# A one-core hybrid decoder step: one down sum per group, down loads two steps ahead, earlier first weights, preloaded residual rows

## The chip, the core and the metric

The kernel runs on one core of a Trainium2 chip. A core has five engines with queues of their own: the TensorE (PE; weight loads show as PEld) multiplies matrices into PSUM, the VectorE (DVE), the ScalarE (ACT) and GpSimd (POOL) work on elements, and the SyncE (SP) here issues every DMA. Each engine takes its instructions in a fixed order; what it reads from another engine or from a DMA it waits for by a semaphore. The metric is the device time of one execution in microseconds (us); lower is better.

## What is computed

One step of a decoder layer on 1104 tokens: 16 learned meta tokens and a prompt of 1024 as one sequence, and 8 samples of 8 tokens. A token mixer (a gated short convolution and a state-space part) is followed by an output projection, and then a feed-forward block (FFN). The end of the layer is what matters here:

```python
    mix = jnp.concatenate([ya, yb], axis=-1) @ w_out
    h = h + rmsnorm(mix, norm_mix_post)
    fn = rmsnorm(h, norm_ffn_pre)
    f = (jax.nn.silu(fn @ w_gate) * (fn @ w_up)) @ w_down
    h = h + rmsnorm(f, norm_ffn_post)
```

All is float32; the width is 1024, the FFN's 2816.

## The kernel before

**Products.** A float32 matrix product is made of three products of rounded halves: an operand is split into `hi` (an ACT copy into a rounded type) and `lo` (operand minus `hi`, a `tensor_tensor` on DVE or POOL), and PE computes hi·hi + hi·lo + lo·hi. So each weight needs a load, an ACT copy and a subtraction ahead of its use.

**Order of instructions.** A planner orders each engine's queue at build time, by its own estimate of times and by priorities: an instruction's place in the program, moved ahead by n places within `tc.high_priority(offset=n)`. Tiles of a pool with the same `tag` share `bufs` slots; a tile waits until the slot's last user is done. A pool that is opened after another was closed takes over its memory and waits for the tiles that lay there. The order is fixed on the chip: an instruction at the head of a queue holds everything behind it.

**Stages that the change touches.**

1. *Output projection* (lines 923 to 959). Three groups of token tiles, `GROUPS = ((1, 2, 3), (4, 9, 5), (6, 7, 8))`; tiles 1 to 8 are 128 prompt tokens each, 9 the samples. For each group twelve slices of `w_out` are loaded (`wo`), scaled and split (`woh`, `wol`) and multiplied. `load_mix` loads and splits the other operand (`mhb`, `mlb` and so on). After a group `h_tile` copies its sums out of PSUM; `residual` norms them and adds the input rows (line 868); `fn_tile` norms again, transposes on PE and fills `xr` and `B1`, the FFN's input. Both run within the next group; those of the last group run with the first FFN products.
2. *FFN up* (lines 964 to 1150). Gate and up weights (`g`, `u`) are taken in `NQ = 11` groups of 256 columns. A fast scheme for block matrices (Strassen, Winograd's form) makes seven products of 2 × 2 blocks: `first(q)` computes the products with B11 and B21 (two each for g and u), `rest(q)` the other five (T2, T3, T1, T4, B22; ten with g and u). The combinations of input blocks, the *B sums*, are made once (lines 1127 to 1137), those of the weights by `sums` in each group. `first` runs ahead for groups 0 to 2 (`ND = 3`) with weights of its own from `early_weights`; from group 3 on it is part of the group. PE's row "yg L982 <- DVE u2g" is a wait in `rest`: the accumulator Y is read by the DVE (`u2`, `u3`, lines 1048 and 1052) before the next product is added to it.
3. *Down sums* (`down_sums`, lines 1088 to 1097). For each group 1 MB of `w_down` is loaded into `xr[q % 2][0]` (row `xr<-in_w_down_dram`), POOL makes four sums in place, and the result is stored in DRAM as `d_t[q]`.
4. *Down projection* (lines 1154 to 1339): 42 steps, seven products with six batches of blocks each, in the order 1, 2, 6, 7, 4, 5, 3. `load(i)` loads and splits step i's operands; `draw()` hands out four half buffers in turn. Products 6, 7, 4 and 5 read `d_t`.
5. *Finish* (`finish_half`): a sum of squares on ACT, the product with the weight of the norm, the power −0.5 on POOL, and for each half row the residual `d_h` loaded into one of three buffers, added and stored.

## Time and profile before

| | us |
|---|---|
| median of 3 runs | 1493.08 (1485.3 to 1493.22) |
| the profiled execution | 1492.86 |
| its span, first to last instruction | 1490.9 |
| TensorE busy | 1399.4 |
| DVE, ACT, POOL busy | 921.0, 607.7, 563.2 |
| mean granted clock of the TensorE | 0.980 |

In the rows of the profile `L982 PE MATMUL xg<-B01h,a11g` means line 982, engine, operation, what it writes and what it reads, buffer numbers left out. A row of a group ends with the count, the busy time and the mean nanoseconds of one, and behind the last bar with the idle time ahead of it and what ended that. A row of the timeline begins with the start and the duration; brackets hold the idle time ahead of it and its releaser. In a row of stretches each engine has its busy time and, in parentheses, its instructions; then come the granted clock (1.00 is full), the mean share of time that the DMA engines were busy, and GB/s.

### The profile page before, as it was taken

The page shows a single profiled execution, that of the slowest core. Times are in us where ns is not written, and L with a number is a line of the kernel's source. Part 1 is how long each engine was busy: PE and PEld are TensorE (multiplying, and loading weights), DVE is VectorE, ACT ScalarE, POOL GpSimd, SP SyncE. Part 2 cuts the span into 40 slices and gives each one's busy share as a digit, 9 for nine tenths or more (in the row PEclk, how much of TensorE's full clock was granted, in tenths as well). Part 3 has the DMA queues.
Part 4 walks back from the last instruction along what each step waited for, and adds up shares of the span by engine and source line. Part 5 has one row for each costly group of instructions (what it writes and reads, how often), then busy time and mean ns, then how long its engine had stood idle before and what let it go on. Part 6 is the DMA issues. An engine that isn't in the chain of part 4 may idle for free.

```text
span 1490.9 us, 22203 instructions
## 1 busy us (share of the span) xinstructions
PE 1399.4 (94%) x8837; PEld 1267.5 (85%) x8837; DVE 921.0 (62%) x1050; ACT 607.7 (41%) x966; POOL 563.2 (38%) x404
## 2 busy tenths in 40 slices
PE   5999998989999889999989898999999999899996
PEld 5899987878898777787879888999999998687885
DVE  6555455656666976577499786665665545345654
ACT  5465444334433544565454222333333334343331
POOL 3122133434344453221157677222222233344442
PEclk9999999999999999999999999999999999999998
DMA  7143247667646557864434777432322357555445
GB/s 215 46 117 102 89 130 192 186 157 207 167 130 170 141 150 245 255 214 162 151 114 163 277 277 270 137 99 89 101 87 73 109 146 243 180 169 180 166 166 190
DMA packets 243696, 240.98 MB, mean 162 GB/s; under 512 B 32589, under 2 KB 193441, under 8 KB 242185
## 3 DMA queue, kind: packets, MB, share of 16 engines
q1 hardware_dynamic: 243592, 239.57, 51.5%
q8 instruction: 69, 1.13, 0.3%
q14 instruction: 35, 0.28, 0.1%
HBM read 170.81 MB, written 68.72 MB: 161 GB/s over the span
## 4 chain that ended last, share of the span: by engine, by line
PE 42%; DVE 6%; DMA 4%; issue 3%; ACT 2%; POOL 1%; SPq 0%; DVEq 0%; ACTq 0%; POOLq 0%
PE d L1306 11%; PE o L949 6%; PE yg L982 5%; PE yu L982 5%; PE xu L982 4%; PE xg L982 3%; PE zg L982 3%; PE zu L982 3%; DMA wg<-in_w_gate_dram 1%; DMA wu<-in_w_up_dram 1%; DMA c_p<-d_h 1%; PE d1s L1317 0%; DMA c_h<-d_h 0%; PE fT L896 0%; DVE c_p L1250 0%
## 5 line engine op out<-in xcount | busy, mean ns | idle before, releaser
L105 POOL TENSOR_TENSOR wd<-draw,wd 128x1024 fp32r<-128x1024 f32 (+1 forms) x41 | 98.8, 2413 | 118.8 <-ACT wd L1185 101.8
L218 PE MATMUL px<-xh,whi 128*128 128x272 f32 (+2 forms) x288 | 95.5, 333 | 0.0
L219 PE MATMUL px<-xl,whi 128*128 128x272 f32 (+2 forms) x288 | 94.9, 330 | 0.0
L220 PE MATMUL px<-xh,wlo 128*128 128x448 f32 (+2 forms) x288 | 94.2, 331 | 0.0
L105 POOL TENSOR_TENSOR wlo<-raw,whi 128x1024 fp32r<-128x1024 f32 x20 | 50.4, 2518 | 78.3 <-ACT whi L113 78.2
L252 DVE SCALAR_TENSOR_TENSOR xa<-xr,vec,xa 128x1040 f32<-128x1040 f32 x72 | 56.8, 846 | 33.9 <-issue 25.2
L941 DVE SCALAR_TENSOR_TENSOR wol<-wo,vec,woh 128x1024 fp32r<-128x1024 f32 x34 | 44.1, 1299 | 50.6 <-ACT woh L940 50.6
L1185 ACT ACTIVATE wd<-draw 128x1024 fp32r<-128x1024 f32 (+1 forms) x42 | 41.2, 984 | 80.5 <-DMA draw<-d_t 28.9
L218 PE MATMUL pz<-xh,whi 128*128 128x256 f32 (+2 forms) x192 | 67.7, 353 | 0.8 <-DVE z L594 0.7
L113 ACT ACTIVATE whi<-raw 128x1024 fp32r<-128x1024 f32 x38 | 40.1, 1055 | 62.0 <-PE px L219 20.3
L219 PE MATMUL pz<-xl,whi 128*128 128x256 f32 (+2 forms) x192 | 64.8, 338 | 0.0
L220 PE MATMUL pz<-xh,wlo 128*128 128x256 f32 (+2 forms) x192 | 64.8, 338 | 0.0
L940 ACT ACTIVATE woh<-wo,vec 128x1024 fp32r<-128x1024 f32 x34 | 38.8, 1148 | 45.5 <-PE o L949 44.4
L1306 PE MATMUL d<-wd,B01h 128*128 128x512 f32 x176 | 55.6, 396 | 0.0
L219 PEld LDWEIGHTS px<-xl,whi 128*128 128x128 f32 x288 | 54.1, 188 | 1.6
L218 PEld LDWEIGHTS px<-xh,whi 128*128 128x128 f32 x288 | 54.2, 188 | 1.4
L220 PEld LDWEIGHTS px<-xh,wlo 128*128 128x128 f32 x288 | 53.8, 188 | 1.7 <-issue 0.2
L105 DVE TENSOR_TENSOR wlo<-raw,whi 128x1024 fp32r<-128x1024 f32 x18 | 27.8, 1547 | 38.1 <-ACT whi L113 38.1
L1306 PE MATMUL d<-wd,T3h 128*128 128x512 f32 x152 | 47.6, 392 | 3.5 <-ACT c_p L1267 2.0
L949 PE MATMUL o<-wol,mhb 128*128 128x512 f32 x144 | 46.2, 406 | 3.0 <-DVE wol L941 2.0
L975 POOL TENSOR_TENSOR s3u<-wu,s3u 128x512 fp32r<-128x512 f32 x11 | 20.2, 1836 | 70.4 <-ACT s3u L974 70.4
L1306 PE MATMUL d<-wd,B11h 128*128 128x512 f32 x144 | 45.2, 396 | 0.0
(590 smaller groups left out, 4521.8 us busy)
## 6 DMA issues: line engine op xcount, KB each, us to landing
wo<-in_w_out_dram SPq DMA_DIRECT2D x36, 512.0 KB, 3.9
draw<-d_a SPq DMA_DIRECT2D x35, 512.0 KB, 4.3
raw<-in_w_in_dram SPq DMA_DIRECT2D x32, 512.0 KB, 5.3
wg<-in_w_gate_dram SPq DMA_DIRECT2D x11, 1024.0 KB, 5.3
wu<-in_w_up_dram SPq DMA_DIRECT2D x11, 1024.0 KB, 5.3
xr<-in_w_down_dram SPq DMA_DIRECT2D x11, 1024.0 KB, 7.2
d_t<-xr SPq DMA_DIRECT2D x11, 1024.0 KB, 7.9
draw<-d_t SPq DMA_DIRECT2D x20, 512.0 KB, 4.6
```

Source lines behind the costliest of these rows:

```text
L105: eng.tensor_tensor(out=out, in0=a, in1=hi.bitcast(F32), op=ALU.subtract)
L113: S.activation(hi[:, :], raw[:, :], AF.Copy)
L218: PE.matmul(acc, hi[:, wk], xh[t][:, k, o:], start=k == 0, stop=False)
L219: PE.matmul(acc, hi[:, wk], xl[t][:, k, o:], start=False, stop=False)
L220: PE.matmul(acc, lo[:, wk], xh[t][:, k, o:], start=False, stop=k == KD - 1)
L252: V.scalar_tensor_tensor(out=dst, in0=src(i), scalar=wv[:, wcol(i):wcol(i) + 1], in1=dst, op0=ALU.mult, op1=ALU.add)
L940: S.activation(hi, raw, AF.Copy, scale=nv)
L941: V.scalar_tensor_tensor(out=lo, in0=raw, scalar=nv, in1=hi[:, :].bitcast(F32), op0=ALU.mult, op1=ALU.subtract)
L949: PE.matmul(accs[i][c], l[:, kb, :], r_[:, c * 512:(c + 1) * 512], start=n == 0 and q == 0, stop=n == 11 and q == len(steps) - 1)
L982: PE.matmul(acc[:, c, 0:W1], w_[l][k], b[r_][:, k, c * W1:(c + 1) * W1], start=start and k == 0 and x == 0, stop=k == 3 and x == 2, skip_g ...
L1185: S.activation(hi, x, AF.Copy)
L1306: PE.matmul(accs[t], sx[x][:, tl], wx[y], start=st and x + y == 0, stop=en and x == 1, skip_group_check=n not in OPENS)
```

## The change

The edits are these.

- *Down sums*: `down_sums(0)` runs ahead of the loop over groups, `down_sums(q + 1)` after `rest(q)`. `rest(q)` puts its difference `s2` into `xr[(q + 1) % 2][0]` instead of the tile `p5`; the next round loads there.
- *First weights*: `early_weights` of group 0 is called in the last output-projection group after step 9, with tiles of the mix operands (`mhb`, `mlb`) for its halves. Those of groups 1 and 2 use the pool `pw`, which opens after `first(0)`. `first(1)` follows the B sums in the program, then come the loads and sums of group 0 and `first(2)`. `f` of group 1 lies in the block b22.
- *B sums*: no raised priority; the split of B22 goes from POOL to DVE, that of T3 from DVE to POOL.
- *Output projection*: loads and splits of `w_out` have a priority 300 places ahead; the residual add of the first two groups is on POOL; `load_mix` takes the tiles in sorted order (4, 5, 9).
- *Down projection*: step i calls `load(i + 2)` instead of `load(i + 1)`.
- *Finish*: in the last step the residual rows of tiles 1 to 4 are loaded into the raw buffers, and `finish_half` adds in place there; the second half's product with the norm's weight goes to `c_u3` for these tiles.

```diff
-HP4, HP5 = 300, 1000
+HP4, HP5, HPW = 300, 1000, 300
...
-        V.tensor_tensor(out=h[:w], in0=h[:w], in1=xt[:w], op=ALU.add)
+        (V if i in GROUPS[-1] else G).tensor_tensor(out=h[:w], in0=h[:w], in1=xt[:w], op=ALU.add)
...
-        for i in tiles:
+        for i in sorted(tiles):
...
+    def early_weights(x, q):
+
+        src = WG[x][:, 2 * q * P:(2 * q + 1) * P].rearrange("(k p) m -> p k m", p=P)
+        eng = V if x == "g" else G
+        if q == 0:
+            raw = wp.tile([P, KD * P], F32, tag="raw", name=f"we{x}", bufs=3)[:, :].rearrange("p (k m) -> p k m", m=P)
+            hi, lo = (pm.tile([P, KD, P], F32R, tag=f"m{y}b", name=f"we{x}{y}", bufs=4)[:, :, :] for y in "hl")
+        else:
+            raw = pw_[0].tile([P, KD, 2 * P], F32, tag="raw", name=f"we{x}{q}", bufs=2)[:, 0:4, :]
+            raw = raw.rearrange("p k (a m) -> p (k a) m", m=P)
+            hi, lo = (pw_[0].tile([P, 2, 4, P], F32R, tag="w", name=f"we{x}{q}{y}", bufs=8)[:, :, :, :]
+                      .rearrange("p a k m -> p (a k) m") for y in "hl")
+        SY.dma_start(raw, src)
+        S.activation(hi, raw, AF.Copy)
+        eng.tensor_tensor(out=lo, in0=raw, in1=hi.bitcast(F32), op=ALU.subtract)
...
-            raw = wp.tile([P, DM], F32, tag="raw", name=f"wo{k}", bufs=3)
-            SY.dma_start(raw, w_out[k * P:(k + 1) * P, :])
+            with tc.high_priority(offset=HPW):
+                raw = wp.tile([P, DM], F32, tag="raw", name=f"wo{k}", bufs=3)
+                SY.dma_start(raw, w_out[k * P:(k + 1) * P, :])
...
+            if n == 9 and gi + 1 == len(GROUPS):
+                for x in "gu":
+                    early_weights(x, 0)
...
-        f = ptile("f11", f"f11{q}")
+        f = two(xr[1][1][:, 0, :]) if q == 1 else ptile("f11", f"f11{q}")
...
-        a12, a21, a22, s2 = (flat(t)[:, 0:NH] for t in (p1s["u", q], u2["u"], u3["u"], p5["g"]))
+        a12, a21, a22, s2 = (flat(t)[:, 0:NH] for t in (p1s["u", q], u2["u"], u3["u"], xr[(q + 1) % 2][0][:, :, :]))
...
-    for q in range(ND):
-        first(q)
-        if q == 0:
-            with tc.high_priority(offset=HP4):
-                for args in pend:
-                    fn_tile(*args)
+    first(0)
+    with tc.high_priority(offset=HP4):
+        for args in pend:
+            fn_tile(*args)
...
-    with tc.high_priority(offset=HP5):
-        (b11, b12), (b21, b22) = xr
-        V.tensor_tensor(out=b11, in0=b12, in1=b11, op=ALU.subtract)
-        G.tensor_tensor(out=b12, in0=b22, in1=b12, op=ALU.subtract)
-        bsplit(B22, b22, G)
-        V.tensor_tensor(out=b22, in0=b22, in1=b11, op=ALU.subtract)
-        bsplit(T2, b22, V)
-        bsplit(T3, b12, V)
...
+    (b11, b12), (b21, b22) = xr
+    for x in "gu":
+        early_weights(x, 1)
+    V.tensor_tensor(out=b11, in0=b12, in1=b11, op=ALU.subtract)
+    bsplit(B22, b22, V)
+    G.tensor_tensor(out=b12, in0=b22, in1=b12, op=ALU.subtract)
+    V.tensor_tensor(out=b22, in0=b22, in1=b11, op=ALU.subtract)
+    bsplit(T2, b22, V)
+    bsplit(T3, b12, G)
...
+    first(1)
+    for x in "gu":
+        early_weights(x, 2)
+    A0 = {x: wraw(x, 0) for x in "gu"}
+    ws0 = {x: sums(x, 0, A0[x]) for x in "gu"}
+    first(2)
...
+    down_sums(0)
     for q in range(NQ):
-        As = {x: wraw(x, q) for x in "gu"}
+        if q:
+            As = {x: wraw(x, q) for x in "gu"}
...
-        rest(q, As, a11)
-        down_sums(q)
+        rest(q, {x: sums(x, q, As[x]) for x in "gu"} if q else ws0, a11)
+        if q + 1 < NQ:
+            down_sums(q + 1)
...
-        V.tensor_tensor(out=dst, in0=dst, in1=fpost[:w, cs], op=ALU.mult)
+        if c == 1 and 1 <= i <= 4:
+            part[i, c] = c_u3[:, i - 1, :]
+        V.tensor_tensor(out=part[i, c], in0=dst, in1=fpost[:w, cs], op=ALU.mult)
...
-            ht = hts[hturn[0] % 3]
-            hturn[0] += 1
-            SY.dma_start(ht[:w], d_h[i][:, qs])
+            if 1 <= i <= 4:
+                ht = hlast[i][:, qs]
+            else:
+                ht = hts[hturn[0] % 3]
+                hturn[0] += 1
+                SY.dma_start(ht[:w], d_h[i][:, qs])
...
-        if i and i + 1 < len(steps):
-            load(i + 1)
+        if i + 2 < len(steps):
+            load(i + 2)
...
+        if i + 1 == len(steps):
+            for t in range(4):
+                hlast[t + 1] = draw()
+                SY.dma_start(hlast[t + 1], d_h[t + 1][:, :])
```

More of the change, by code (lines that the diff above doesn't have):

```diff
@@ L921, in load_mix @@
             mix[part, i] = mh, ml
+    WG = {"g": w_gate, "u": w_up}
+    early = {}
+    def early_weights(x, q):
[12 more added lines that the diff above has]
+        eng.tensor_tensor(out=lo, in0=raw, in1=hi.bitcast(F32), op=ALU.subtract)
+        early[x, q] = [[[t[:, k, :] for k in range(4 * h, 4 * h + 4)] for t in (hi, lo)] for h in range(2)]
+    pw_ = []
     turn[0] = 0
@@ L930, in hymba_kernel @@
             nv = vec[:, 72 + k:73 + k]
-            raw = wp.tile([P, DM], F32, tag="raw", name=f"wo{k}", bufs=3)
-            SY.dma_start(raw, w_out[k * P:(k + 1) * P, :])
-            hi = wp.tile([P, DM], F32R, tag="whi", name=f"woh{k}", bufs=2)
-            lo = wp.tile([P, DM], F32R, tag="wlo", name=f"wol{k}", bufs=2)
-            if (tiles[0], n) in WOG:
-                S.activation(raw, raw, AF.Copy, scale=nv)
-                S.activation(hi, raw, AF.Copy)
-                G.tensor_tensor(out=lo, in0=raw, in1=hi[:, :].bitcast(F32), op=ALU.subtract)
-            else:
-                S.activation(hi, raw, AF.Copy, scale=nv)
-                V.scalar_tensor_tensor(out=lo, in0=raw, scalar=nv, in1=hi[:, :].bitcast(F32), op0=ALU.mult,
-                                       op1=ALU.subtract)
+            with tc.high_priority(offset=HPW):
+                raw = wp.tile([P, DM], F32, tag="raw", name=f"wo{k}", bufs=3)
+                SY.dma_start(raw, w_out[k * P:(k + 1) * P, :])
+                hi = wp.tile([P, DM], F32R, tag="whi", name=f"woh{k}", bufs=2)
+                lo = wp.tile([P, DM], F32R, tag="wlo", name=f"wol{k}", bufs=2)
+                if (tiles[0], n) in WOG:
+                    S.activation(raw, raw, AF.Copy, scale=nv)
+                    S.activation(hi, raw, AF.Copy)
+                    G.tensor_tensor(out=lo, in0=raw, in1=hi[:, :].bitcast(F32), op=ALU.subtract)
+                else:
+                    S.activation(hi, raw, AF.Copy, scale=nv)
+                    V.scalar_tensor_tensor(out=lo, in0=raw, scalar=nv, in1=hi[:, :].bitcast(F32), op0=ALU.mult,
+                                           op1=ALU.subtract)
             for i in tiles:
@@ L1008, in first @@
             if As is None:
-                ws[x] = early_weights(x, q)
+                ws[x] = early[x, q]
             else:
@@ L1038, in sums, with rest @@
         return w6, w7, w5, w4, w3
-    def rest(q, As, a11):
-        ws = {x: sums(x, q, As[x]) for x in "gu"}
+    def rest(q, ws, a11):
         Y = {x: pacc(f"y{x}{q}") for x in "gu"}
```

16 lines of the change are left out of this document (7 added, 9 removed).

## The prediction

> **What bounds the kernel now.** I read the page's busy shares first, then busy time by stage, then what the TensorE waited for.
>
> ```profile
> PE 1399.4 (94%) x8837; PEld 1267.5 (85%) x8837; DVE 921.0 (62%) x1050; ACT 607.7 (41%) x966; POOL 563.2 (38%) x404
> ```
> ```profile
> core 0: us, PE busy (x) PEld busy (x) DVE busy (x) ACT busy (x) POOL busy (x), PEclk, DMA share, GB/s
> 0.00:567.00 567.00, 525.80 (x3399) 473.14 (x3399) 349.39 (x454) 260.40 (x453) 204.50 (x185) 0.98 0.53 149
> 567.00:734.60 167.60, 159.70 (x707) 129.32 (x707) 100.99 (x105) 85.00 (x120) 37.98 (x29) 0.98 0.64 205
> 734.60:790.90 56.30, 45.67 (x317) 43.89 (x316) 51.43 (x40) 31.84 (x45) 32.24 (x14) 0.91 0.38 121
> 790.90:892.80 101.90, 92.66 (x719) 91.94 (x718) 82.46 (x79) 29.18 (x45) 74.31 (x49) 0.97 0.71 252
> 892.80:941.10 48.30, 44.26 (x339) 43.88 (x339) 32.96 (x36) 12.49 (x22) 32.56 (x23) 0.96 0.65 236
> 941.10:1236.10 295.00, 295.00 (x2354) 294.99 (x2353) 173.49 (x220) 97.69 (x157) 80.36 (x57) 1.00 0.33 105
> 1236.10:1477.70 241.60, 236.31 (x1012) 190.39 (x1010) 123.19 (x110) 89.83 (x123) 99.26 (x46) 0.99 0.56 185
> 1477.70:1490.90 13.20, 0.03 (x1) 0.00 (x0) 7.12 (x13) 1.27 (x4) 2.01 (x3) 0.68 0.58 199
> ```
>
> The TensorE (PE) is the bound, and the change takes no matmul away. What can be won is its idle time plus the time at a lower granted clock: length minus busy, plus (1 − PEclk) × length. The rows are: up to the output projection; output projection; the first products of groups 0 to 2 (`first`) with the B sums; groups 0 to 2; group 3; groups 4 to 10; down projection; tail. The loss is 10.6 + 5.1 = 15.7 us in the third, 9.2 + 3.1 = 12.3 in the fourth, 4.0 + 1.9 = 5.9 in the fifth and none in the sixth: 295 / 7 = 42.1 us a group, with nothing to gain. The down stage loses 5.3 + 2.4, the tail is 13.2 us without PE, and the output projection loses 7.9 idle plus some 3.
>
> ```profile
> PE yg L982 <- DVE u2g L1048: 11.4, 3, 5.8
> PE xg L982 <- DVE wlo L105: 4.7, 1, 4.7
> PE xu L982 <- POOL wlo L105: 1.9, 1, 1.9
> PE o L949 <- ACT h L855: 2.8, 1, 2.8
> PE o L949 <- DVE wol L941: 2.0, 1, 2.0
> ```
>
> The waits of the PE name VectorE (DVE) far more than anything else. Why the DVE is late shows at the longest wait:
>
> ```profile
> 820.20 0.38 SPq L969 DMA_DIRECT2D wg<-in_w_gate_dram  x1
> 820.67 0.54 SPq L1091 DMA_DIRECT2D xr<-in_w_down_dram  x1
> 826.12 0.69 DVE L1029 TENSOR_TENSOR wg<-wg 128x512 f32<-128x512 f32 x1 [3.02 <-DMA wg<-in_w_gate_dram]
> 832.17 0.71 DVE L1048 TENSOR_TENSOR u2g<-yg,p1g 128x544 f32<-128x544 f32 x1
> 832.94 0.82 PE L982 MATMUL yg<-T3h,s3g 128*128 128x272 f32 x2 [5.84 <-DVE u2g L1048]
> ```
>
> The DVE sits before the next group's weights, whose load shares its time with a down load; the read of Y that the PE needs (`u2g`) is queued behind. And the down sums are all here:
>
> ```profile
> L1093 POOL TENSOR_TENSOR xr<-xr 128x512 f32<-128x512 f32 x11 | 16.0, 1455 | 30.2 <-DMA xr<-in_w_down_dram 30.2
> 800.80 1.29 POOL L1093 TENSOR_TENSOR xr<-xr 128x512 f32<-128x512 f32 x1 [3.78 <-DMA xr<-in_w_down_dram]
> 922.82 1.36 POOL L1093 TENSOR_TENSOR xr<-xr 128x512 f32<-128x512 f32 x1 [1.07 <-DMA xr<-in_w_down_dram]
> xr<-in_w_down_dram SPq DMA_DIRECT2D x11, 1024.0 KB, 7.2
> d_t<-xr SPq DMA_DIRECT2D x11, 1024.0 KB, 7.9
> ```
>
> Eleven rounds of four GpSimd (POOL) sums of about 1.5 us run from 801 to 928, each with a load and a store of 1 MB, though their products come in the down stage, after 1236. What POOL does costs the DVE too:
>
> ```profile
> 759.29 5.25 POOL L1130 TENSOR_TENSOR xr<-xr,xr 128x2176 f32<-128x2176 f32 x1 [3.55 <-ACT xr L898]
> 759.80 5.28 DVE L1033 TENSOR_TENSOR wg<-sg,wg 128x512 f32<-128x512 f32 x1
> 785.77 0.68 DVE L1033 TENSOR_TENSOR wu<-su,wu 128x512 f32<-128x512 f32 x1
> ```
>
> The same DVE subtraction takes 0.68 us alone and 5.28 beside a POOL sum, ending as POOL ends. I therefore add both engines' SBUF-only operations as if they shared one lane. The Trainium skill, SBUF — State Buffer, section "Who interferes with whom", says this as a rule: a DVE instruction with two SBUF inputs and a GpSimd one that reads SBUF lock each other out for a whole instruction. These rows agree.
>
> **Down sums, one per group.** Round q+1 now loads into the buffer through which `rest(q)` stores `s2`, so it can't start before that group's end. From 790.9 to 941.1 ten to eleven rounds become four. Lane work of one group without `first`, in the short times of single rows: DVE 14 weight operations and 4 differences of 0.68, three products of about 0.7 (14.4 us; the reads of PSUM, 0.72 each, I leave out, as the row at 832.17 shows one unstretched), POOL 4 splits and 2 adds of about 1.3 (7.8) and one round (6.0): 28.2 us, against 10 products of 3.01 = 30.1 of PE. It fits, tightly. Of the 12.3 + 5.9 = 18.2 us lost there I take back **12** and leave 6, because 94% of a lane still makes queues; bounds 4 and 18. Groups 4 to 10 (14 products each) get a round that they did not have:
>
> ```profile
> 1079.70:1121.80 42.10, 42.10 (x338) 42.10 (x337) 24.90 (x33) 13.40 (x22) 10.88 (x8) 1.00 0.29 96
> 947.41 3.01 PE xg L982 x24
> ```
>
> 24.9 + 10.9 + 6.0 = 41.8 of 42.1 us if the DVE's PSUM reads are counted as lane work, some 35 without them: I cost it at **0**, covered by that slack; without cover it is the slower rival. New waits: the DVE's `s2` waits for round q−1's store, two groups (60 us at least) after that round's load; load 7.2, sums 6.0 and store 7.9 us are 21, so it costs nothing. SP holds round q+1's load until `s2` is stored; behind it stand the next group's weights, which wait for the same group's splits anyway.
>
> **First weights and B sums.** Group 0's two splits move into the output projection, on tiles that are free by step 9: two loads on SP among the last output weights', where they stand now already, two ACT copies of 1.06, a DVE and a POOL operation (1.2, 2.5). The 1.87 us wait of `xu` goes. What is late next is the norm of the last tokens:
>
> ```profile
> 737.05 3.06 POOL L105 TENSOR_TENSOR wlo<-raw,whi 128x1024 fp32r<-128x1024 f32 x1 [0.47 <-ACT whi L113]
> 737.93 3.26 DVE L868 TENSOR_TENSOR h<-h,xt 128x1024 f32<-128x1024 f32 x1
> 752.23 1.28 DVE L884 SCALAR_TENSOR_TENSOR hn<-h,hr8r,ffn_bc 128x1024 f32<-128x1024 f32 x1
> L105 POOL TENSOR_TENSOR wlo<-raw,whi 128x1024 fp32r<-128x1024 f32 x20 | 50.4, 2518 | 78.3 <-ACT whi L113 78.2
> ```
>
> Group 1's splits now live in a later pool, on memory that this norm frees: not before 753.5, less some 2 us since the stretched sum at 737.93 (1.2 elsewhere) is gone. Then ACT 1.06 and DVE 1.2 or POOL 2.5: `first(1)` starts between 754 and 758, against 754.6 now, so the PE idles some 5 us after `first(0)`, but `first(2)` need not wait 4.7 us. Two times 12 us give 778 to 782 instead of 788.4 (790.9 less the 2.5 us by which `yg` and `yu` had run ahead, with their waits). Lane work up to T2: 3.8 (splits 1) + 9.7 + 5.3 (b11, B22, b22, T2; b12) + 3.8 + 4.1 (splits 2, three weight operations each for g and u) = 26.7, from about 752.5: 779, just in time. T3, T1 and T4 come out 1 to 3 us late by the same sum. Group 1's `f` goes into b22, and waits for the DVE's b21; what it holds is PSUM that `rest(0)` wants later still: 0. I take **8**; bounds 0 and 14.
>
> **Output projection.**
>
> ```profile
> L941 DVE SCALAR_TENSOR_TENSOR wol<-wo,vec,woh 128x1024 fp32r<-128x1024 f32 x34 | 44.1, 1299 | 50.6 <-ACT woh L940 50.6
> ```
>
> Six adds of 1.2 us leave the DVE for POOL, where 1024 elements take 2.5; weights go ahead of norms in every queue. The PE's 2.0 us for `wol` came behind norms on the DVE; that should go, and half of this stage's 3 us of slow clock with it. The opposite cost is the wait on `h` L855 (2.8 us): evictions may now queue behind a split of 1.15. By the Trainium skill's rule above, the moved adds would block `wol` for up to 2.4 us each; taking 7 us more lane time as all on the path would turn this term into a loss of some 4. The row says that the DVE idled 50.6 us ahead of the splits, 1.5 each, so most of that has cover and I don't follow it: **3**, bounds −5 (the two waits of 2.8 and 2.0 once more) and 6 (both gone, with some clock). Sorted loads of group 2: 0, the operands are there a step early.
>
> **Down loads two steps ahead**: the same 84 loads; the buffers (two raw, four split) still limit them, and a split issued earlier may also stand before an eviction. Of 7.7 us **2**, bounds −3 and 6.
>
> **Tail.**
>
> ```profile
> 1477.34 0.39 PE L1306 MATMUL d<-wd,B01l 128*128 128x512 f32 x1
> 1481.49 0.68 DVE L1282 TENSOR_TENSOR c_u<-d,c_u 128x512 f32<-128x512 f32 x1
> 1484.00 0.55 POOL L1244 TENSOR_TENSOR fr<-fs,mhalf 128x1 f32<-128x1 f32 x1 [4.11 <-DVE fs L1241]
> 1485.68 0.75 DVE L1250 SCALAR_TENSOR_TENSOR c_p<-c_u,fr,c_p 128x512 f32<-128x512 f32 x1 [1.83 <-DMA c_p<-d_h]
> 1487.20 0.99 SPq L1251 DMA_DIRECT2D out_dram<-c_h  x2
> ```
>
> The last eviction stands 3.8 us behind tile 3's results on the DVE, and 1.1 us go to the row load. The rows of tiles 1 to 4 now load in four transfers into the raw buffers, once the last step's weights are split; they land while the last products run, and replace eight loads on SP. So: 0.7 evict, 0.9 square, 0.3 scale, 0.9 power, 1.5 two results, then the 3.1 from the end of the last result (1487.84) to 1490.9 as now: 7.4 instead of 13.2. Something for queues: **5**, bounds 3 and 6.
>
> **Sum.** 12 + 8 + 3 + 2 + 5 = 30. The profiled execution took 1492.86 us (1490.9 span and 2.0 around it), 0.2 below the median 1493.08. Forecast **1463 us**.
>
> **Rivals.**
> - *The lane stays full* (0.15): the four rounds and the B sums still queue before `u2g`; only tail, down and output projection gain, with a third of the rest: 10 + 7 = 17 us, 1476. For it: 94%. Against: the long waits were begun by loads.
> - *Late memory* (0.12): group 1's loads too wait for the norm: 3.7 us load + 1.06 + 2.5 after 753.5 is 761; `first(2)` ends as late as now, the 8 us are gone: 1471.
> - *Slower* (0.07): in groups 4 to 10 a POOL sum holds the DVE and `u2g` comes after its slack of 3.4 us (the PE's other products between). At the wait of 832.94 that cost 5.8, and some 1.7 of clock (the fourth and fifth rows lost 5.0 in three such waits); 7 groups × 7.5 = 53, less 30: 1516. It decides from 5.4 us a group (37.5 / 7).
> - *It does not do what it says* (0.08): the order comes from a planner's own estimate of times, so weights ahead and loads ahead change nothing, a projection's weights lose their place to the output weights, and the gain is 5 of tail and a few: 1486.
>
> **How the numbers follow.** Forecast 0.58; its own range, half way to the sums of all bounds (gains of 50 and −1, so 40 and 14), is 1453 to 1479. With the lane (0.15) and the late memory (0.12) inside and half of the last case, 1452 to 1486 holds some 0.8; the slower case and what lies past an edge stay out. A measurement can tell about 0.5% (7.5 us) from no change: faster 0.82, same 0.10 (most of "does not do", a little of the lane), slower 0.08.
>
> The Trainium skill, TensorE: Matmul & The Clock Gate, Part 1, has the clock halved after an idle window of about 3.4 us; 0.91 of 56.3 us is 10 us at half, so that rule fits these rows and would repay each short wait removed by up to 1.7.
>
> **What would show it.** Right: POOL's L1093 spread evenly, one each 30 to 42 us; no PE wait over 2 us on `u2g`; no PE wait on `wol`; 8 to 9 us after the last matmul. Wrong: PE waits in groups 4 to 10; DVE and POOL above 95% together before 890; `first(1)` starting after 760.

## The result, and the profile after

| | before | changed |
|---|---|---|
| median of 13 runs each | 1490.48 us | 1478.40 us |
| lowest and highest | 1485.3, 1495.04 | 1472.85, 1486.53 |
| profiled execution, its span | 1492.86, 1490.9 | 1475.88, 1474.1 |
| ratio of the times | | 0.9925, 95% interval 0.9902 to 0.9947 |

The change gains 12.1 us by the medians (0.8%), where 30 were forecast. The two profiled executions lie 17.0 us apart, because the one before is 2.4 us above its median and the one after 2.5 below its own. The page after, busy shares:

```profile
PE 1390.7 (94%) x8837; PEld 1260.7 (86%) x8837; DVE 924.8 (63%) x1044; ACT 609.7 (41%) x966; POOL 577.2 (39%) x410
```

They look as before. The stretches tell more. First those of the changed kernel: output projection, from the first product of `first(0)` to the end of `rest(0)` (called *group 0* from here on), groups 1 to 3, groups 4 to 10, down projection, tail. The columns are those of the prediction's table.

```profile
561.00:727.10 166.10, 158.40 (x708) 128.03 (x707) 98.97 (x99) 85.30 (x121) 59.32 (x36) 0.99 0.63 204
727.10:819.70 92.60, 73.32 (x555) 71.58 (x555) 76.90 (x65) 42.84 (x59) 44.35 (x23) 0.89 0.41 137
819.70:928.50 108.80, 104.56 (x819) 103.91 (x818) 77.41 (x90) 31.97 (x53) 46.42 (x32) 0.98 0.45 159
928.50:1225.90 297.40, 296.03 (x2353) 294.96 (x2353) 192.32 (x217) 96.24 (x155) 123.65 (x85) 1.00 0.45 151
1225.90:1466.50 240.60, 232.78 (x1012) 190.23 (x1010) 128.47 (x117) 91.70 (x125) 98.52 (x48) 0.99 0.59 193
1466.50:1474.10 7.60, 0.00 (x0) 0.00 (x0) 3.66 (x7) 0.72 (x2) 0.55 (x1) 0.70 0.49 188
```

The same stretches of the kernel before, cut at the end of group 0 (the others stand in the prediction):

```profile
734.60:820.70 86.10, 75.47 (x555) 73.69 (x554) 77.56 (x62) 43.26 (x60) 54.56 (x28) 0.94 0.41 138
820.70:941.10 120.40, 107.12 (x819) 106.01 (x818) 89.29 (x93) 30.25 (x52) 84.55 (x57) 0.96 0.74 266
```

Subtracting stretch by stretch: 7.5 us are won up to the first product (734.6 to 727.1), 11.6 in groups 1 to 3, 1.0 in the down projection and 5.6 in the tail; 2.4 are lost in groups 4 to 10 and **6.5 in group 0**. That is 16.8, the difference of the spans. So group 0 ends only 1.0 us earlier, although the projection ahead of it ended 7.5 earlier. What the TensorE waited for between 561 and 1230 us in the changed kernel (total, times, longest):

```profile
PE xg L1006 <- DVE weg1l L940: 11.3, 1, 11.3
PE xg L1006 <- ACT weg1h L939: 5.7, 1, 5.7
PE yg L1006 <- DVE u2g L1065: 5.4, 5, 2.1
PE o L972 <- ACT woh L963: 3.2, 2, 1.6
PE o L972 <- DVE wol L964: 1.8, 1, 1.8
```

The waits on `u2g` (11.4 us before) have shrunk, and a new one of 11.3 us stands at the top: `first(1)` waits for the low half of its gate weights, `weg1l`, after it has waited 5.7 us for the high half, `weg1h`. The timeline of the changed kernel shows what stood ahead of it:

```profile
742.96 0.40 SPq L938 DMA_DIRECT2D weg<-in_w_gate_dram  x1
745.42 4.80 POOL L1148 TENSOR_TENSOR xr<-xr,xr 128x2176 f32<-128x2176 f32 x1 [6.01 <-DVE xr L1146]
746.37 6.14 DVE L1141 TENSOR_TENSOR B22l<-xr,B22h 128x2176 fp32r<-128x2176 f32 x1 [1.09 <-ACT B22h L1140]
748.15 1.04 ACT L939 ACTIVATE weg1h<-weg 128x1024 fp32r<-128x1024 f32 x1
750.21 4.49 POOL L940 TENSOR_TENSOR weu1l<-weu,weu1h 128x1024 fp32r<-128x1024 f32 x1
752.43 4.55 DVE L1141 TENSOR_TENSOR T1l<-xr,T1h 128x2176 fp32r<-128x2176 f32 x1
754.67 6.94 POOL L1141 TENSOR_TENSOR T3l<-xr,T3h 128x2176 fp32r<-128x2176 f32 x1
756.91 5.78 DVE L940 TENSOR_TENSOR weg1l<-weg,weg1h 128x1024 fp32r<-128x1024 f32 x1
```

Its operands were there at 749.2, but the DVE did two input blocks first, B22 and T1, which `rest(0)` needs last and third. And the two engines take strict turns here. From the ends of these rows: b12 on POOL ends at 750.22, B22l on the DVE at 752.51, `weu1l` on POOL at 754.70, T1l on the DVE at 756.98, T3l on POOL at 761.61, `weg1l` on the DVE at 762.69. Each comes 2.29, 2.19, 2.28, 4.63 and 1.08 us after the other engine's end, about its own unstretched duration (on the DVE 2.42 for 2176 elements and 1.22 for 1024; on POOL 2.39 for 1024 and some 4.8 for 2176). A subtraction of 1.2 us took 5.78. The tail is as planned; the last operations after the last matmul:

```profile
1467.16 0.68 DVE L1315 TENSOR_TENSOR c_u<-d,c_u 128x512 f32<-128x512 f32 x1
1470.33 0.74 DVE L1281 SCALAR_TENSOR_TENSOR draw<-c_u,fr,draw 128x512 f32<-128x512 f32 x1
```

The last eviction starts 0.7 us after the last matmul instead of 3.8, and the results no longer wait for rows.

### The profile page after: what moved, and what is told of

Its sections match the earlier page's. It is cut to its first block, busy times and chain, and to the rows that moved or that the text cites. A ratio compares the mean times of both kernels' runs of the same rounds, so it can differ in the third digit from the quotient of the medians.

```text
span 1474.1 us, 22183 instructions
## 1 busy us (share of the span) xinstructions
PE 1390.7 (94%) x8837; PEld 1260.7 (86%) x8837; DVE 924.8 (63%) x1044; ACT 609.7 (41%) x966; POOL 577.2 (39%) x410
## 4 chain that ended last, share of the span: by engine, by line
PE 52%; DVE 16%; DMA 16%; issue 6%; ACT 5%; POOL 3%; SPq 1%; DVEq 0%; POOLq 0%; ACTq 0%
PE d L1339 9%; PE o L972 6%; PE yg L1006 4%; PE yu L1006 4%; PE zu L1006 3%; DMA wg<-in_w_gate_dram 3%; PE zg L1006 3%; PE px L218 3%; PE px L220 3%; PE px L219 3%; DMA M<-d_a 3%; PE xg L1006 2%; PE xu L1006 2%; DMA draw<-d_a 2%; DMA mra<-d_ya 1%
## 5 line engine op out<-in xcount | busy, mean ns | idle before, releaser
L105 POOL TENSOR_TENSOR wd<-draw,wd 128x1024 fp32r<-128x1024 f32 (+1 forms) x40 | 94.9, 2373 | 113.5 <-ACT wd L1211 113.4
L105 POOL TENSOR_TENSOR wlo<-raw,whi 128x1024 fp32r<-128x1024 f32 x17 | 41.7, 2453 | 77.8 <-ACT whi L113 77.7
L964 DVE SCALAR_TENSOR_TENSOR wol<-wo,vec,woh 128x1024 fp32r<-128x1024 f32 x34 | 47.9, 1413 | 36.6 <-ACT woh L963 36.6
L113 ACT ACTIVATE whi<-raw 128x1024 fp32r<-128x1024 f32 x32 | 33.8, 1055 | 58.5 <-PE px L219 20.8
L1110 POOL TENSOR_TENSOR xr<-xr 128x512 f32<-128x512 f32 x11 | 14.8, 1346 | 106.8 <-DMA xr<-in_w_down_dram 95.8
L1339 PE MATMUL d<-wd,T2h 128*128 128x512 f32 x144 | 45.0, 396 | 0.0
```

Of the source, the lines that this page charges most:

```text
L105: eng.tensor_tensor(out=out, in0=a, in1=hi.bitcast(F32), op=ALU.subtract)
L113: S.activation(hi[:, :], raw[:, :], AF.Copy)
L964: V.scalar_tensor_tensor(out=lo, in0=raw, scalar=nv, in1=hi[:, :].bitcast(F32), op0=ALU.mult, op1=ALU.subtract)
L1339: PE.matmul(accs[t], sx[x][:, tl], wx[y], start=st and x + y == 0, stop=en and x == 1, skip_group_check=n not in OPENS)
```

## The experiments

The table has the medians of the thirteen kernels, their ratios to runs of the kernel before on the same chip, and from each profile: when the first FFN product started, and the length of the stretches (us).

| kernel | median | ratio, 95% interval | first product | group 0 | groups 1–3 | groups 4–10 | down | tail |
|---|---|---|---|---|---|---|---|---|
| before | 1490.5 | | 734.6 | 86.1 | 120.4 | 295.0 | 241.6 | 13.2 |
| changed | 1478.4 | 0.9925, 0.9902–0.9947 | 727.1 | 92.6 | 108.8 | 297.4 | 240.6 | 7.6 |
| e1_hold | 1476.3 | 0.9894, 0.9860–0.9928 | 727.1 | 91.6 | 109.8 | 300.2 | 238.8 | 7.7 |
| e2_alldve | 1477.8 | 0.9897, 0.9861–0.9933 | 731.2 | 90.7 | 110.1 | 299.1 | 244.1 | 7.6 |
| e3_w1early | 1480.5 | 0.9918, 0.9886–0.9951 | 721.2 | 88.0 | 110.5 | 298.9 | 243.3 | 7.7 |
| e4_oldfirst | 1472.3 | 0.9852, 0.9830–0.9874 | 725.9 | 83.8 | 112.4 | 300.3 | 241.0 | 7.6 |
| e5_hold_t14 | 1471.9 | 0.9868, 0.9835–0.9900 | 720.3 | 84.2 | 113.3 | 299.4 | 240.2 | 7.7 |
| e6_old_bsums_dve | 1470.7 | 0.9831, 0.9791–0.9871 | 722.1 | 79.5 | 113.8 | 298.0 | 237.4 | 7.7 |
| e7_old_down_dve | 1467.6 | 0.9828, 0.9799–0.9856 | 731.2 | 83.7 | 106.5 | 297.8 | 240.6 | 7.7 |
| e8_before_chain | 1491.8 | 0.9996, 0.9973–1.0018 | 736.5 | 84.9 | 113.5 | 300.8 | 242.4 | 13.8 |
| e9_both_dve | 1464.0 | 0.9820, 0.9793–0.9846 | 731.4 | 79.5 | 109.3 | 297.8 | 242.2 | 7.7 |
| e10_no_pool | 1453.3 | 0.9756, 0.9730–0.9781 | 723.9 | 77.3 | 102.9 | 294.5 | 242.1 | 7.5 |
| e11_unchained | 1460.5 | 0.9796, 0.9771–0.9820 | 730.2 | 79.8 | 109.3 | 294.8 | 235.3 | 7.7 |
| e12_no_pool_unchained | 1449.3 | 0.9749, 0.9722–0.9776 | 723.3 | 78.5 | 102.7 | 294.7 | 238.3 | 7.6 |
| e13_before_no_pool | 1468.6 | 0.9861, 0.9833–0.9890 | 734.5 | 81.9 | 102.3 | 294.9 | 239.7 | 13.7 |

One profile's first product and down stage scatter by many us between kernels with the same code there (720 to 731, 235 to 244); group 0 and groups 1 to 3 scatter by one or two, groups 4 to 10 by up to three. Each length is from one profile, so a difference of 1 or 2 us in one stretch can't be told from scatter. The argument goes by these stretches, and the totals by the medians.

### Is it the order on the DVE? e1_hold

```diff
     V.tensor_tensor(out=b11, in0=b12, in1=b11, op=ALU.subtract)
+    wl = early["g", 1][0][1][0]
+    V.tensor_copy(out=T1[0][:, 0, 0:1], in_=wl[:, 0:1])
+    V.tensor_copy(out=B22[1][:, 0, 0:1], in_=wl[:, 0:1])
     bsplit(B22, b22, V)
```

> The changed kernel, with the splits of T1 and B22 held behind the DVE's split of group 1's gate weights (two one-element copies make them wait). From the first product of first(0) to the first product of rest(0) the changed kernel's profile has 55.0 us (727.1 to 782.1), the one before 49.8. Theory A, order: weg1l is late only because B22l and T1l stand ahead of it on the DVE, where it was ready at 749.2; so it ends near 751 (24 us after the first product instead of 35.6), the wait of 11.3 us on it falls to 2, and the stage to 48 or 49 us: a total some 6 to 8 us below the changed kernel, about 1471. Rival B, the lane: DVE and POOL together have the same work to do up to T2l, some 31 us from the start of the B sums, so the wait only moves to T2l and the stage stays at 53 to 55 us, total as the changed kernel's, 1478. Rival C, late memory: weg1l comes late whatever its place, because its load is: the wait stays over 8 us.

The wait on `weg1l` fell to 2.1 us, as theory A has it, and the stage up to `rest(0)` took 53.6 us, as rival B has it; group 0 got only 1.0 us shorter, no more than scatter. Group 0 in e1_hold, and its longest waits of the TensorE:

```profile
727.10:818.70 91.60, 77.30 (x555) 74.90 (x555) 78.22 (x67) 43.27 (x59) 44.59 (x23) 0.91 0.41 139
```
```profile
PE xg L1006 <- ACT weg1h L939: 4.5, 1, 4.5
PE yg L1006 <- ACT s2g L998: 2.3, 1, 2.3
PE xg L1006 <- DVE weg2l L940: 2.2, 1, 2.2
PE xg L1006 <- DVE weg1l L940: 2.1, 1, 2.1
PE yu L1006 <- DVE s2u L999: 2.0, 1, 2.0
```

The wait on `weg1h` stayed (5.7 us before, 4.5 now). The one of 11.3 became four of about 2, on the weights that come next. Idle time in the stretch fell from 19.3 to 14.3 us (length less busy), and the busy time of the same 555 matmuls rose from 73.3 to 77.3: the low clock, which in the changed kernel fell mostly into the long wait (granted 0.50 all through it), now falls on matmuls. So order alone gave 5.0 and the clock took back 4.0.

### Is it a shared lane? e2_alldve and e3_w1early

e2_alldve gives POOL's part of this stretch to the DVE:

```diff
-    G.tensor_tensor(out=b12, in0=b22, in1=b12, op=ALU.subtract)
+    V.tensor_tensor(out=b12, in0=b22, in1=b12, op=ALU.subtract)
-    bsplit(T3, b12, G)
+    bsplit(T3, b12, V)
...
-        eng = V if x == "g" else G
+        eng = V if x == "g" or q else G
```

> The changed kernel, with all B sums and all early splits of groups 1 and 2 on the DVE, none on POOL. Theory L, one lane: DVE operations of 128x2176 take 2.42 us each instead of 6.14, 4.55 and 3.52 (B22l, T1l, T4l), as nothing runs on POOL beside them; weg1l, though now fifth in its queue, ends 11 us after the B sums' start (19.9 in the changed kernel), the stage from the first product to rest(0) shrinks from 55.0 to 51 or 53 us, total 1474 to 1476. Rival P, two engines in parallel, the long DVE operations being slowed by something else (DMA traffic, ACT): they stay at 4 to 6 us, and with 18 us of POOL work added the DVE is later, the stage 60 us or more, total 1484 or above.

The timeline of e2_alldve, DVE and POOL:

```profile
751.80 2.42 DVE L1141 TENSOR_TENSOR B22l<-xr,B22h 128x2176 fp32r<-128x2176 f32 x1
754.13 2.42 DVE L1141 TENSOR_TENSOR T1l<-xr,T1h 128x2176 fp32r<-128x2176 f32 x1
756.47 1.22 DVE L940 TENSOR_TENSOR weg1l<-weg,weg1h 128x1024 fp32r<-128x1024 f32 x1
...
765.07 8.85 POOL L1110 TENSOR_TENSOR xr<-xr 128x512 f32<-128x512 f32 x1 [21.59 <-DMA xr<-in_w_down_dram]
765.75 2.42 DVE L1141 TENSOR_TENSOR T2l<-xr,T2h 128x2176 fp32r<-128x2176 f32 x1
...
774.00 1.29 POOL L1111 TENSOR_TENSOR xr<-xr 128x512 f32<-128x512 f32 x1
```

With POOL idle the same three operations take 2.42, 2.42 and 1.22 us instead of 6.14, 4.55 and 5.78, and `weg1l` ends 10.8 us after the B sums' start, with one more large operation ahead of it, instead of 19.8. The stretching came from POOL. The other way round, POOL's sum of 1.29 us took 8.85 while the DVE worked without a pause. The rival of two parallel engines is out. Group 0 still got only 1.9 us shorter, and the median, 1477.8 us, missed theory L's 1474 to 1476 and is the changed kernel's within the noise. Its up weights' load is queued on SP behind the store of the first down round, which waits for POOL's held-off sums:

```profile
778.72 0.34 SPq L1114 DMA_DIRECT2D d_t<-xr  x1
779.16 0.38 SPq L993 DMA_DIRECT2D wu<-in_w_up_dram  x1
787.78 0.69 DVE L1047 TENSOR_TENSOR wu<-wu 128x512 f32<-128x512 f32 x1 [4.53 <-DMA wu<-in_w_up_dram]
```

The DVE, with its other work done, stood idle for 4.5 us until they had landed.

In e3_w1early group 1's weights are split in the output projection too.

```diff
-        if q == 0:
-            raw = wp.tile([P, KD * P], F32, tag="raw", name=f"we{x}", bufs=3)[:, :].rearrange("p (k m) -> p k m", m=P)
+        if q < 2:
+            raw = (wp.tile(...) if q == 0 else pm.tile([P, KD, P], F32, tag="mrb", name=f"we{x}{q}", bufs=2)[:, :, :])
...
                 for x in "gu":
                     early_weights(x, 0)
+                for x in "gu":
+                    early_weights(x, 1)
```

> The changed kernel, with group 1's weights also loaded and split within the output projection, on mixer tiles that are free there. Theory A, order and lane: first(1) follows first(0) without a wait; the wait goes to group 2's split, which stands behind b11, T1l, B22l and b22 on the DVE and ends 16 to 21 us after the B sums' start; the stage from the first product to rest(0) is 43 to 48 us instead of 55.0, total 1467 to 1472. Rival D: two more splits (1.2 on DVE, 2.4 on POOL, two copies on ACT) at the end of the output projection delay the evictions and output weights there, and B sums and T tiles that lie on these mixer tiles wait for first(1): the stage or the projection gets longer by as much, total 1476 to 1480.

`first(1)` followed without a wait, and then `first(2)` waited 2.9 and 5.4 us for its weights and `rest(0)` 2.1 for `s2g`. The stretch up to `rest(0)` took 53.8 us, and theory A's 43 to 48 was wrong: B22l on the DVE and T3h on ACT waited 2.2 and 3.3 us until the products of `first(1)` had freed the mixer tiles (rival D's point), the copy `weg2h` stood behind T3h, and the split `weg2l` took 5.82 us beside POOL's T3l (6.93). Group 0 came to 88.0, 4.6 less than in the changed kernel, but the median didn't fall.

### Undoing the rearrangement: e4_oldfirst and e5_hold_t14

e4_oldfirst has the weights of groups 1 and 2 and the B sums as before the change.

```diff
+    for q in (1, 2):
+        for x in "gu":
+            early_weights(x, q)
+        first(q)
     phx.__exit__(None, None, None)
...
-    for x in "gu":
-        early_weights(x, 1)
+    with tc.high_priority(offset=HP5):
...
-    bsplit(B22, b22, V)
+        bsplit(B22, b22, G)
-    bsplit(T3, b12, G)
+        bsplit(T3, b12, V)
...
-    first(1)
-    for x in "gu":
-        early_weights(x, 2)
-    first(2)
```

> The changed kernel, with the weights of groups 1 and 2 and the B sums as in the kernel before (weights on the old buffers ahead of the B sums, sums at raised priority, B22's split on POOL, T3's on DVE); group 0's weights stay within the output projection. Theory A, that this rearrangement is what cost the forecast gain: the stage from the first product to rest(0) is 46 to 50 us instead of 55.0, the wait for weg1l is under 3 us, total 1471 to 1474. Rival R: the old arrangement is no better once the projection has ended 7 us earlier, since the norm of the last tokens and the lane set the time: stage 53 to 56 us, total 1477 to 1480.

Theory A: the stage up to `rest(0)` takes 48.9 us, group 0 takes 83.8, 8.8 less than in the changed kernel, and the interval of the ratio lies wholly below the changed kernel's. So this part of the change costs more than it brings, though not all of the 8.8 us are won: groups 1 to 10 are 6.5 us longer in its profile, and the median is some 6 us lower.

e5_hold_t14 keeps the new arrangement, with e1's order, and takes T1 and T4 out of the way instead.

```diff
+    wl = early["g", 1][0][1][0]
+    V.tensor_copy(out=B22[1][:, 0, 0:1], in_=wl[:, 0:1])
     bsplit(B22, b22, V)
...
-    bsplit(T1, b11, V)
-    bsplit(T4, b21, V)
...
     ws0 = {x: sums(x, 0, A0[x]) for x in "gu"}
+    wl = ws0["u"][0][1][0]
+    V.tensor_copy(out=T1[0][:, 0, 0:1], in_=wl[:, 0:1])
+    V.tensor_copy(out=T4[0][:, 0, 0:1], in_=wl[:, 0:1])
+    bsplit(T1, b11, V)
+    bsplit(T4, b21, V)
     first(2)
```

> As e1_hold (group 1's split ahead of B22's), and T1 and T4 are split only after group 0's own weights, so that the first round of down sums, which uses T1's source, comes after them too. From the first product of first(0) to the end of rest(0)'s products it was 92.6 us in the changed kernel, 91.6 in e1_hold, 83.8 in e4_oldfirst, 86.1 before. Theory A, the lane's content: some 11 us of lane work (T1l and T4l 2.4 each, a round of down sums 6) that no product needs before rest(0) leave the stretch ahead of group 0's splits; the stage comes to 82 to 86 us, the total to 1468 to 1472. Rival M, the two raw buffers: group 0's gate and up weights are loaded only when group 2's splits have freed the buffers (issued at 771 and 778 in the changed kernel, 753 in the one before), so s2u still comes near 62 us after the first product and the stage stays at 88 to 92, total 1475 to 1478.

84.2 us: theory A. Work for later products, ahead of work for the next one, was the loss: once the splits of T1 and T4 and the first round of down sums are out of the way, the new arrangement does as well as the old one (83.8). How much each of the three is worth was not run. The raw buffers didn't decide here.

### Which engine: e6_old_bsums_dve and e7_old_down_dve

The timeline of e4_oldfirst explains what was left:

```profile
753.62 5.31 POOL L1144 TENSOR_TENSOR B22l<-xr,B22h 128x2176 fp32r<-128x2176 f32 x1
754.24 5.24 DVE L1050 TENSOR_TENSOR wg<-sg,wg 128x512 f32<-128x512 f32 x1
```

Small DVE operations again wait out POOL's large ones. e6_old_bsums_dve moves those two to the DVE, on top of e4_oldfirst:

```diff
-        G.tensor_tensor(out=b12, in0=b22, in1=b12, op=ALU.subtract)
-        bsplit(B22, b22, G)
+        V.tensor_tensor(out=b12, in0=b22, in1=b12, op=ALU.subtract)
+        bsplit(B22, b22, V)
```

> As e4_oldfirst, with the B sums' b12 and B22 split on the DVE instead of POOL. In e4_oldfirst the wait of 6.3 us for group 2's gate split ends when the DVE reaches it behind three operations of 0.7 us that took 5.3 each beside POOL's b12 and B22l. Theory L, one lane: the two sums take 2.4 us each instead of 5.0 and 5.3, the wait falls to 0 to 2.5 us, the stage from the first product to the end of rest(0) from 83.8 to 78 to 81, the total to 1466 to 1470. Rival P, parallel engines: the DVE gets 4.8 us more, the wait stays above 5 us, the stage at 84 to 89, total 1472 to 1477.

Group 0 of e6_old_bsums_dve:

```profile
722.10:801.60 79.50, 73.38 (x555) 71.93 (x554) 72.58 (x64) 41.65 (x58) 32.35 (x21) 0.96 0.36 124
```

4.3 us less, inside the bracket of the lane, from giving the busier engine more to do. The total doesn't show it by itself: the intervals of the two ratios overlap.

e7_old_down_dve does the same to the down sums, on top of e4_oldfirst:

```diff
-        G.tensor_tensor(out=b11, in0=b12, in1=b11, op=ALU.subtract)
+        V.tensor_tensor(out=b11, in0=b12, in1=b11, op=ALU.subtract)
```

(and so the other three sums.)

> As e4_oldfirst, with the rounds of down sums on the DVE instead of POOL (four sums of 0.68 us instead of four of 1.35 that hold the DVE as long). Theory L, one lane: groups 4 to 10, 300.3 us in e4_oldfirst and 295.0 before the change, come back to 295 to 297; groups 1 to 3 (112.4) lose their three waits on u2g (2.3, 1.5, 2.5) wholly or in part: 106 to 110; total 1464 to 1468. Rival Q, the queue: 2.7 us a group more stand before u2g on the DVE, the waits on u2g grow to 3 us or more and appear in groups 4 to 10: 302 us or more there, total 1474 to 1480.

Groups 1 to 3 fell from 112.4 to 106.5, groups 4 to 10 from 300.3 to 297.8, a little above the bracket; the median, 1467.6 us, is inside its own.

### What is the chain worth? e8_before_chain, e9_both_dve and e11_unchained

e8_before_chain is the kernel before with the chain alone:

```diff
-... (p1s["u", q], u2["u"], u3["u"], p5["g"]))
+... (p1s["u", q], u2["u"], u3["u"], xr[(q + 1) % 2][0][:, :, :]))
...
+    down_sums(0)
     for q in range(NQ):
...
-        down_sums(q)
+        if q + 1 < NQ:
+            down_sums(q + 1)
```

> The kernel before with one part of the change alone: the down sums chained one per group, with rest(q)'s s2 in their buffer. Theory A, that this part gave the gain of groups 1 to 3 by itself: these take 108 to 111 us instead of 120.4, groups 4 to 10 take 296 to 300 instead of 295.0, the rest stays; total 7 to 11 us below the kernel before. Rival S: groups 1 to 3 were shortened by what the B sums' rearrangement left over (T1 and T4 split earlier), not by the chain: they stay at 116 to 120, groups 4 to 10 lose 2 to 5, total within 3 us of the kernel before or above it.

Its groups 1 to 3 and 4 to 10:

```profile
821.40:934.90 113.50, 106.10 (x818) 105.44 (x818) 78.28 (x91) 31.93 (x53) 45.74 (x32) 0.97 0.45 159
934.90:1235.70 300.80, 296.50 (x2353) 295.18 (x2352) 193.43 (x217) 96.03 (x155) 122.36 (x85) 1.00 0.44 150
```

6.9 us won and 5.8 given back, a ratio of 0.9996: neither theory has both numbers, and the total is the rival's. The seven rounds that left the first groups now run in groups that had no idle time, and the TensorE waits there four times for `u2g`, 4.3 us in all.

e9_both_dve joins e6 and e7, and e11_unchained takes the chain out of it again (the edit of e8 reversed).

> e6_old_bsums_dve and e7_old_down_dve together: the old arrangement of the first weights, all B sums and all down sums on the DVE, the chain, the tail and the output projection as in the changed kernel. If both effects come from the lane that DVE and POOL share, they add: the stage from the first product to the end of rest(0) 78 to 81 us (79.5 in e6), groups 1 to 3 105 to 108 (106.5 in e7, 113.8 in e6), groups 4 to 10 296 to 299; total 1458 to 1464, ratio to the kernel before 0.977 to 0.982. Rival: the down sums on the DVE stand ahead of the weights' splits that the first one has brought forward, and one gain eats the other: groups 1 to 3 stay at 110 or more, total 1466 to 1470.

Group 0 and groups 4 to 10 came as expected; groups 1 to 3, at 109.3, stayed above the bracket: of the 4.2 us that group 0 ends sooner than in e7, 2.8 are missing here.

> As e9_both_dve without the chain: rest(q) stores s2 from its own buffer again and the rounds of down sums run as early as their loads allow, on the DVE. Theory A, the chain is worth its gain wherever the rounds run: eleven rounds of 2.7 us come together in groups 0 to 3, some 8 us a group ahead of u2g, groups 0 to 3 together 8 to 15 us longer than in e9_both_dve, groups 4 to 10 back at 295; total 4 to 10 us above. Rival: with the rounds at 2.7 us instead of 6, spreading them is worth nothing: groups 0 to 10 together within 3 us of e9_both_dve, total the same.

Its groups 1 to 3 and 4 to 10:

```profile
810.00:919.30 109.30, 103.23 (x818) 102.43 (x818) 97.03 (x129) 30.95 (x52) 33.31 (x21) 1.00 0.80 287
919.30:1214.10 294.80, 294.80 (x2354) 294.79 (x2353) 173.34 (x220) 96.74 (x156) 78.64 (x57) 1.00 0.33 105
```

The rival: packed into the first groups, the rounds cost them nothing, and groups 4 to 10 run without a gap. Groups 0 to 10 take 483.9 us against 486.6 with the chain. So over all groups the place of the sums mattered little on either engine (2.7 us here in favour of the early place; in e8 6.9 won and 5.8 given back), and the engine more: from e4 to e7 the same rounds in the same place got groups 1 to 10 8.4 us shorter.

### To the end: e10_no_pool, e12_no_pool_unchained and e13_before_no_pool

e10_no_pool is e9_both_dve with all splits of the FFN's up weights on the DVE.

```diff
-        eng = V if x == "g" else G
+        eng = V
...
-        w7 = wsplit(a21, f"s3{x}{q}", G)
+        w7 = wsplit(a21, f"s3{x}{q}", V)
-        w4 = wsplit(a22, f"a22{x}{q}", G)
+        w4 = wsplit(a22, f"a22{x}{q}", V)
```

(and so the second block in `first`.)

> As e9_both_dve, with the weights' splits of all groups on the DVE too, so that POOL keeps two additions a group. Theory L, one lane, carried to its end: a split costs 0.68 us instead of 1.3 to 1.7 of the lane, four a group (six with first), the waits on u2g go down again: groups 1 to 3 102 to 106 us, groups 4 to 10 295 to 297, total 2 to 5 us below e9_both_dve. Rival Q, the queue: reads of PSUM and of DMA'd weights run beside POOL without loss, so taking work from POOL only makes the DVE's queue longer ahead of u2g: groups 1 to 3 108 or more, waits of 2 us and more, total 2 to 8 us above e9_both_dve.

Its groups 1 to 3 and 4 to 10, and what the TensorE waited for on `u2g` from 720 to 1210 us:

```profile
801.20:904.10 102.90, 102.51 (x819) 102.29 (x818) 79.25 (x116) 31.78 (x52) 9.64 (x6) 1.00 0.49 174
904.10:1198.60 294.50, 294.50 (x2353) 294.50 (x2353) 200.34 (x284) 96.23 (x155) 27.98 (x18) 1.00 0.45 152
```
```profile
PE yg L1005 <- DVE u2g L1064: 0.4, 1, 0.4
```

The lane theory holds to its end, and by more than expected: 10.7 us below e9_both_dve. e12_no_pool_unchained takes the chain out of it as well.

> As e10_no_pool without the chain of the down sums. Theory C, the chain is worth nothing once POOL no longer holds the DVE, and costs some 6 us at the down stage's start, where e11_unchained took 235.5 us against 242.5 in e9_both_dve and 242.2 in e10_no_pool: groups 0 to 3 together 180 to 184 us (180.2 in e10), groups 4 to 10 295, down stage 235 to 238, total 1446 to 1451, ratio 0.971 to 0.975. Rival K: the down stage's 235.5 was luck of that one profile, and the rounds packed into groups 0 to 3 cost 4 us or more there: down stage 240 to 243, total 1453 to 1460.

1449.3 us, as theory C has it; but its ratio and e10's overlap almost wholly, and the down stage's 238.3 lies within what other kernels scatter. Whether the chain costs anything there stays open. They are 25 and 29 us faster than the changed kernel by the medians.

e13_before_no_pool is the kernel before with the engine changed in the same five places, and nothing else.

> The kernel before, with nothing of the change, but the B sums, the down sums and all weights' splits of the feed-forward groups on the DVE. Theory L, one lane: POOL's holding of the DVE was the cause of the waits that the change was costed against, so without any other part group 0 (86.1 us from the first product to the end of rest(0)) takes 77 to 81, groups 1 to 3 (120.4) 103 to 109, groups 4 to 10 stay at 295; tail and output projection stay; total 1466 to 1473, some 20 us below the kernel before and below the changed kernel. Rival: the other parts are needed as well (the chain for groups 1 to 3, the rearranged first weights): group 0 stays above 84 or groups 1 to 3 above 114, total 1478 to 1490.

Its group 0 and groups 1 to 3:

```profile
734.50:816.40 81.90, 74.75 (x555) 73.28 (x554) 73.08 (x82) 43.69 (x61) 8.06 (x8) 0.94 0.45 152
816.40:918.70 102.30, 102.30 (x818) 102.17 (x817) 95.04 (x143) 31.92 (x53) 9.51 (x6) 1.00 0.86 309
```

Groups 1 to 3 have no idle time at all, though they hold three rounds of down sums each with all their loads. Compare the row of the kernel before: DVE 89.29 and POOL 84.55 busy of 120.4. Doing nearly all of both engines' work alone takes the DVE 95.04 us, hardly more than the 89.29 it took for its own part before. So much of what the page counts as busy was one engine held up by the other. Group 0's 81.9 are a little above the bracket. This one move gains 18.1 us in groups 1 to 3, where the change was forecast to gain 12, and 22 in all. e10, which has the change's other parts beside it except the rearranged B sums, is another 15 us faster by the medians; 6.2 of that are the tail (13.7 to 7.5), and how the rest divides is not shown.

## Why the prediction was wrong

The bound was read rightly: PE, waiting for the DVE, with POOL sharing the DVE's lane. The sum by its terms, against the pair of profiles:

| term | forecast, bounds | measured | |
|---|---|---|---|
| down sums, groups 1 to 3 | 12 (4 to 18) | 11.6 | right size, wrong reason |
| the same, groups 4 to 10 | 0 | −2.4 | loss missed |
| first weights and B sums | 8 (0 to 14) | −6.5 | **wrong sign** |
| output projection | 3 (−5 to 6) | 7.5 | partly scatter |
| down loads two ahead | 2 (−3 to 6) | 1.0 | within scatter |
| tail | 5 (3 to 6) | 5.6 | right |

- **First weights and B sums: the step that failed** is "Then ACT 1.06 and DVE 1.2 or POOL 2.5: `first(1)` starts between 754 and 758". From the first product that is 19.4 to 23.4 us; in the changed kernel `first(1)` gets its low half after 35.6 (762.75). The memory was not late (load issued at 742.96, 15.9 us after the first product, where the prediction had the memory free after 17 to 19), the idle 5 us that the prediction expected behind `first(0)` came (5.7, on `weg1h`), and the split could have been done by 751. The step put the split directly behind its ACT copy and added up the lane's work only up to T2, as if the DVE would take it in the order of need. The DVE took B22, then T1, then the split, whose 1.2 us became 5.78 beside a POOL operation. The amount of work was near: T2's split ended 42.7 us after the first product, where the sum had 44.4. But T1 and T3 were done by then, and group 2's and group 0's weights were not. e1_hold shows that the place of the one split is worth only 1.0 us, e5_hold_t14 that later work ahead of the next product is worth 7.4 more, e6_old_bsums_dve that the engine is worth 4.3 in the old arrangement. This term alone is 14.5 us short, all terms together 13.2; the rest of the miss lies between the pair of profiles (17.0) and the medians (12.1) and belongs to no stage.
- **Down sums.** The 11.6 us agree with the forecast, the cause doesn't, so the agreement is in part luck. The chain alone gives 6.9 in these groups; the rest came only with a long group 0: where group 0 takes 80 to 85 us, groups 1 to 3 take 112 to 114 (e4, e5, e6, e8), where it takes 88 to 93, 109 to 111 (the changed kernel, e1 to e3). No run isolates that exchange. The prediction called the lane 94% full, and moved rounds along it instead of asking why a round costs 6 us. It costs 2.7 on the DVE.
- **Groups 4 to 10.** "I cost it at **0**, covered by that slack": the cover was short, by 0.3 us a group in the changed kernel (2.4 / 7) and 0.8 in e8_before_chain (5.8 / 7), instead of the slower rival's 7.5. Its mechanism is there, with a load in front: ahead of the longest wait on `u2g` in the changed kernel here, 0.5 us at 1033.0, the DVE stood 2.1 us at the next group's weights, and one of their sums then took 1.66 us instead of 0.68 beside a POOL sum. With the rounds on the DVE the stretch stayed at 297.8 (e7, e9); it fell to 294.5 only with the splits there too (e10), and to 294.8 without the chain (e11). So round, splits and loads together filled the slack, and how much is due to each stays open.
- **Output projection.** The waits on `wol` did not go (1.8 us on the row shown); the wait of 2.8 us on `h` did, and waits of 3.2 us on `woh` came. Of the 7.5 us, 6.0 lie in the first row of stretches (567.0 against 561.0), most of which has the same instructions in both kernels. Twelve profiles with the new projection have the first product at 720.3 to 731.4, three with the old one at 734.5 to 736.5; so there is a gain, and its size is not settled.
- **Rivals and signs.** "The lane stays full" (1476 us, given 0.15) was nearest in time, but not in place: the waits on `u2g` fell to 5.4 us and groups 1 to 3 gained 11.6; the lane was in the way in group 0, at `weg1l`. That the time came near it is luck: an unforeseen loss of 6.5 us in group 0 met gains elsewhere of about the size forecast. "Late memory" had the symptom, `first(1)` late, with another cause. All three signs of being wrong came: three waits in groups 4 to 10 (1.2 us in all), `first(1)` after 760, and DVE and POOL above 95% together (77.41 and 46.42 of 108.8 us). The last could not tell, as the kernel before has 89.29 and 84.55 of 120.4. Of the signs of being right, only the spread of the rounds came, one each 31 to 44 us after the first: two waits on `u2g` were just over 2 us, `wol` was still waited for, and the tail was 7.6 us, shorter than the 8 to 9 named.

The rule of the Trainium skill, SBUF — State Buffer, section "Who interferes with whom", was taken as a way of adding durations; e2_alldve agrees with it in both directions (2.42 for 6.14, 8.85 for 1.29). Its consequence for this kernel was not drawn: the lane is shortened by the faster engine.

## What to carry to other kernels

Where DVE and POOL both work on SBUF at the same time, the DVE with two operands there, count them as one lane, at each engine's own duration, and before rearranging the work try it on the faster one: here 0.68 against some 1.3 us for 512 elements. A stretched row is a sign that its engine was held up for part of that time; look for the other engine's operation that ends shortly before it does. When a long wait is broken by reordering, list everything behind it on the same queue that the next products need, since the wait otherwise returns in pieces.
